# A hybrid recurrent layer on one core: odd heads' recurrence products leave TensorE by the upper partitions, and x's squares become two wide instructions

## The chip, the cores and the metric

The kernel runs on one core of a Trainium2 chip. The metric is device time in microseconds, from the start of the program to its end; for one core the slowest core is that core. A core has a matrix engine (TensorE; its weight loads are shown as PEld), a vector engine (VectorE, DVE), a scalar engine (ScalarE, ACT), GpSimd (POOL) and a queue engine (SyncE, SP) that issues DMAs. TensorE writes to PSUM, an accumulator memory of 128 partitions; VectorE and ScalarE copy results from there to SBUF, the working memory, also with 128 partitions. Taking a result out of PSUM is called an eviction below.

## What is computed

One layer (DEPTH is 1) over 512 tokens with 1024 channels. The input is normalised by its root mean square, projected to 6,920 columns, and four token mixers of width 256 run on parts of that projection: gated DeltaNet (GDN), RG-LRU, an S5 state-space layer and RWKV-7. Their outputs are gated, merged, projected and added to x; an MLP with squared ReLU and a final norm follow. What matters here are the norm and the two recurrences over chunks of 64 tokens with four heads of width 64:

```python
def _rmsnorm(x, g):
    y = x32 * lax.rsqrt(jnp.mean(x32 * x32, axis=-1, keepdims=True) + EPS)

# GDN, per chunk
def step(state, inp):
    u_i, w_i, q_i, k_i, a_i, gl_i = inp
    v_new = u_i - jnp.einsum("bhck,bhkv->bhcv", w_i, state)
    o = jnp.einsum("bhck,bhkv->bhcv", q_i, state) + jnp.einsum("bhcj,bhjv->bhcv", a_i, v_new)
    state = state * jnp.exp(gl_i)[..., None, None] + jnp.einsum("bhck,bhcv->bhkv", k_i, v_new)
    return state, o

# RWKV-7, per token (the kernel does it per chunk, too)
def step(state, inp):
    removed = jnp.einsum("bhvk,bhk->bhv", state, kk_t)
    state = (state * w_t[:, :, None, :]
             - jnp.einsum("bhv,bhk->bhvk", removed, kk_t * a_t)
             + jnp.einsum("bhv,bhk->bhvk", v_t, k_t))
    return state, jnp.einsum("bhvk,bhk->bhv", state, r_t)
```

## The kernel before

**Weights and projections.** All weights come as 134 units of 128x1024 fp32. `unit` (L316) loads one, and splits it into a high and a low part: ScalarE writes `hi` as fp32r (L333), VectorE writes `lo`, the rest (L334). `gemm` (L337) then makes each product of three fp32r matmuls (high by high, high by low, low by high). A projection of 128 columns (`proj`, L413) is 24 matmuls of 128x512 into one PSUM bank (`acc`); `nproj` (L419) evicts it on VectorE, scaled by the norm's row `N1["rs"]`. The first six accumulators use banks of their own (EARLY, L222), so that the first projections can be computed before the norm's factor is known.

**The norm.** `norm1` (L406) splits the eight 128x512 tiles of x by `split_g` (L382: `hi` on ScalarE, `lo` on VectorE) and calls `norm_stat` (L345). That squares each tile on ScalarE (L350), adds each square to a sum on VectorE (L354, L357), sums over the partitions by four matmuls with a column of ones (`ssa`, L368; each shows as two instructions), takes the root and the reciprocal (L372, L373), and spreads the result over partitions (`rsa`, L378). Its argument `parts` is 1 in the only call, so `keep_warm` does nothing.

**The RWKV recurrence** (`rwkv_r`, L670) runs over eight chunks. For chunk c, with `rr` the lower or upper 64 partitions for even or odd c: `r1` (L682; called `r` in the profile) multiplies the state `sv` of each head by `ab`, VectorE copies it (L685); `us` (L689) multiplies that by the inverted triangle `tf`, VectorE evicts it negated into the lower half of `uv` (L691), whose upper half is a ScalarE copy of `sv` (L686); `sn` (L696) gives the update of the state, VectorE adds the old state (L697) and multiplies by the decay (L698) into the state of the next chunk; `oT` (L703, L704) gives the output, copied by ScalarE (L705). In `oT` the even heads write the lower 64 partitions and the odd heads the upper 64. In r1, us and sn all four heads write the same 64 partitions, at different columns.

**The GDN recurrence** (`gdn_r`, L930) is built alike: `vn` (L960) and its VectorE copy into `sn` (L963), a ScalarE copy of the state into the other half (L964), the decayed state `sg_` (L967), `sg` (L971) and its addition into the next state (L972), and `oTg` (L977), copied by ScalarE (L978). Here vn and sg write the 64 partitions `rr` for all four heads. The last chunk has no sn, respectively sg.

**Other groups that the text below names.** `s5v` (L1287) are the S5 layer's products with a contraction over 128 partitions, 64 output partitions and 64 columns, whose outputs alternate between lower and upper 64 partitions from one matmul to the next. `s1g` (L916) are GDN's products of keys and queries within a chunk: 64 partitions contracted, 128 columns moving, outputs alternating between the halves. `tri_inverse` (L442) inverts the chunks' triangles: it writes them to DRAM and reads them back in another layout (`scrr` and `scrg`), twice, with a chain of 30 small VectorE instructions between, and has small matmuls of 16 or 32 partitions (`zp`, `t1p`, `z2p`, `z3p`).

**Order.** The PLAN (L68) lists the steps; each has a level of priority and a set of PSUM banks (LV, L63): RWKV's steps and the norm are at level 0, GDN's and S5's at 2. Weight units have a priority of their own, ahead of all levels (L320). From these the framework writes one fixed queue per engine, at build time; an engine works through its queue in order, so an instruction that waits holds up all behind it on that engine.

**Places.** Temporary tiles lie in five regions of SBUF. `al` (L138) gives a tile the place that HOME (L23) names for it, if that is free and of the right type, and otherwise the place that has been free for longest. Two tiles that share a place one after the other are ordered by that: the later one waits for the last reader of the earlier.

Of the kernel before, what the change touches and what calls it, by code (L numbers as in the profile page):

```python
# [22 lines left out]
HOME = {n: [(a[:a.index(":")], int(a[a.index(":") + 1:])) for a in v.split(",")] for n, v in (e.split("=") for e in """  # L23
    xt0=c1b:0 xgh=c0:0 xgl=c0:128 sqa0=c3:650 sqa1=c3:64 sqa2=c3:333 sqa3=c3:618 sqa4=c3:558 sqa5=c1a:81 sqa6=c3:634
    sqa7=c2:185 rsa=c3:202 zero=c2:43,c1b:78 wa=c3:514 gd=c3:64
    px=c2:52,c2:205,c3:383,c3:112,c3:218,c1a:105,c1b:0,c3:488,c3:526,c1b:16,c3:298,c1b:112,c3:525,c1b:16,c2:0,c1b:16
    reset=c3:542 kr=c1b:32 yk=c2:178 svr=c3:0 ab=c2:43 ccb=c1a:59 kf=c3:96,c1a:17 sig=c1b:96,c3:112 af=c3:466,c1b:96
    ei=c1b:112,c1a:0 eia=c1a:80,c3:558 wt=c1a:63,c3:447 bigwup=c3:325 hsbk=c1b:16,c3:298 rf=c3:80,c3:423
    vf=c3:333,c1b:112 rb=c3:349,c3:321 ntr=c1a:64 a2=c3:439 biggup=c2:242 s5s=c3:314 s5pol=c3:134 s5p=c1a:41
    bst=c1a:33 bsx=c2:8 bs2=c3:610 bs3=c3:530 c1=c1a:51 c2=c2:0 bigsb=c3:234 bigsbs=c3:666 bigsc=c2:16 bigscs=c1a:97  # L30
    b8=c3:358 s5t=c3:218,c3:610 s5u=c1a:96 s5ug=c3:325 s5h=c1a:0 lrow=c3:509 gsm=c2:250 ctri=c3:504 qk=c3:96,c3:391
    cv=c1b:0,c3:542,c1b:0,c1b:96,c1a:32,c1a:32 gv=c3:359 lu=c3:542 lh=c1b:96 lr=c1b:0,c1b:16 li=c3:509,c1b:0
    la2=c3:298,c3:298 biglwa=c2:27 biglwx=c2:35 lge=c3:526,c1b:16 c8=c3:218 t8w=c3:138 s5ct=c3:574 s5st=c3:590
    s5am=c2:18 s5ph=c2:175 s5tb=c3:282 s5a=c3:540 s5b=c3:503 s5hs=c3:290 cmr=c3:606 tfr=c2:0 bk=c3:610 s5y=c3:513
    s5yf=c3:326 s5yo=c3:514 bigglu=c1a:48 sgm=c3:290,c3:306 nbr=c1b:87 tnr=c3:128 tmr=c1b:70 tpr=c1b:32 t0tr=c2:210
    ztr=c1b:32 t11tr=c3:574 z2r=c1a:32 ktok=c2:176 ksqg=c1b:64 gpk=c3:136 grows=c3:130 gr=c1a:64 br=c1a:96 eg=c1a:0
    cneg=c2:173 cmg=c2:171 kx=c1b:64 kd=c3:250 svg=c2:176 aq=c3:546 tw=c3:324 ntg=c1a:0 tfg=c3:291 nbg=c1a:40
    tng=c2:35 tmg=c1a:112 tpg=c1a:32 t0tg=c1a:80 ztg=c1a:32 t11tg=c1a:64 z2g=c1a:112
    gt=c1b:0,c1b:0,c1b:16,c3:178,c1b:16,c3:178,c1b:16,c1b:16,c1b:0,c1b:48,c1b:16,c3:185,c1b:16,c1b:16,c3:170,c2:59,c3:234,c1b:0,c3:218,c3:610,c1b:0,c1b:48,c2:75,c2:176,c3:32,c2:0,c3:186,c1b:96,c2:42,c3:513,c1b:16,c2:125,c3:23,c2:32,c3:610,c3:626,c1b:0,c3:580,c3:598,c3:626,c3:337,c3:16,c3:136,c3:64,c3:594,c3:80,c3:626,c3:317
    ofr=c3:128 r1=c3:282,c1b:0,c1b:48,c3:194,c1b:40,c1b:40,c3:505,c1b:40  # L40
    uv=c1b:48,c1b:40,c1b:56,c3:503,c3:168,c3:160,c3:177,c2:34
    sm=c1b:8,c3:194,c1b:40,c3:185,c3:503,c3:168,c3:160,c1b:56 ofg=c2:143
    sn=c3:282,c3:473,c2:117,c3:282,c3:160,c1b:32,c2:92,c3:316
    sgs=c1b:32,c1b:40,c1b:75,c3:315,c3:473,c1b:75,c3:282,c1b:88 osq=c3:658,c3:626 hsbv=c2:16,c3:16 yh1=c1a:32
    yl1=c1a:64 mg=c3:456,c3:497,c3:170,c3:0,c3:48,c3:481,c3:658,c3:234 yh2=c1a:0 yl2=c1a:96 gz=c3:64 q2=c3:530,c1b:112
    o2=c2:240,c3:186 hsbo=c1b:96,c3:513 yh3=c1a:64 yl3=c1a:32 yh0=c1a:96 yl0=c1a:0
    x2=c3:107,c3:642,c3:423,c3:388,c3:407,c3:372,c3:439,c3:290 mh=c2:0 ml=c2:128 h2h=c0:0 h2l=c0:128 sqb0=c3:64
    sqb1=c3:610 sqb2=c3:32 sqb3=c3:0 sqb4=c3:16 sqb5=c3:48 sqb6=c3:531 sqb7=c3:626 rsb=c3:332
    dh=c1a:0,c1b:0,c2:128,c2:0 dl=c2:128,c2:0,c1a:0,c1b:0
    rl=c3:658,c3:0,c3:573,c3:626,c3:20,c3:46,c3:255,c3:0,c3:626,c3:0,c3:594,c3:16,c3:32,c3:56,c3:0,c3:16,c3:16,c3:626,c3:0,c3:32,c3:16,c3:626,c3:156,c3:658,c3:626,c3:610,c3:594,c3:503,c3:626,c3:16,c3:658,c3:0  # L50
    hc0=c3:497 hc1=c3:578 hc2=c3:184 hc3=c3:626 hc4=c3:658 hc5=c3:200 hc6=c3:481 hc7=c3:34 sqc0=c3:513 sqc1=c3:610
    sqc2=c3:236 sqc3=c3:16 sqc4=c3:533 sqc5=c3:610 sqc6=c3:562 sqc7=c3:594 rsc=c3:0
""".split())}
# [47 lines left out]
def trunk(ctx, tc, order, xT, wall, w8, prm, big, cst, gfr, out):  # L101
# [240 lines left out]
                mm(o, a[:, k0 + k, :], b[:, k, :], first and n == 0, last and n == 3 * nk - 1)  # L342
                n += 1

    def norm_stat(xt, nm, parts=1):  # L345
# [13 lines left out]
        def keep_warm(n, t):  # L359
            if parts > 1:  # L360
                w = pa("warm")
                for _ in range(n):
                    mm(w[:, 0:128], ones, t[:, 0:128])
# [2 lines left out]
        for i, acc in enumerate(accs):
            for u in range(4):
                mm(o[:, u:u + 1], acc[:, u * 128:u * 128 + 128], one, i + u == 0, i == parts - 1 and u == 3)  # L368
            keep_warm(3, acc)
        fr(*accs)  # L370
# [559 lines left out]
    def gdn_r():  # L930
# [22 lines left out]
        for c in range(8):  # L953
# [9 lines left out]
            V.tensor_copy(out=sn[rr], in_=o3[rr])  # L963
# [858 lines left out]
```

## Time and profile before

| what | us |
|---|---|
| median of the three runs | 883.51 |
| the three runs | 1213.66, 883.51, 882.94 |
| the profiled execution | 878.68 |
| its span (first instruction to last) | 876.9 |
| granted TensorE clock, mean over the span | 0.991 |

Engine times are sums of busy time within the span. TensorE's busy share counts an instruction until its modelled end, and neighbouring matmuls overlap, so a busy share near 100% doesn't mean that matmuls are as close as they can be; for that the starts of neighbouring matmuls are compared. A matmul on fp32 data (not fp32r) shows as two instructions, with two weight loads. In the timeline a row stands for several equal instructions: start of the first, time from there to the end of the last, count, and in brackets the idle time before and what ended it. The rows of a tile show shortest, median and longest duration in ns. The rows of groups show busy us, mean ns of one, and idle time before.

### The profile page before, as it was taken

What the parts mean: (1) busy time and instruction counts of PE and PEld (TensorE: products, weight loads), DVE (VectorE), ACT (ScalarE), POOL (GpSimd) and SP (SyncE); (2) the same over time, 40 slices, a digit from 0 to 9 for tenths busy, and PEclk for the clock granted to TensorE, in tenths of its full rate; (3) what the DMA queues carried; (4) which work ended last, traced back from release to release, by engine and by line L of the source; (5) the groups of instructions that cost most, each with busy time, mean ns of one, the idle gap of its engine ahead of it and who ended that gap; (6) DMA issues with size and microseconds to landing.
All of it is one profiled execution on the core that took longest, in us unless ns stands there. A gap on an engine that the chain in (4) does not pass through costs nothing.

```text
span 876.9 us, 12992 instructions
## 1 busy us (share of the span) xinstructions
PE 855.5 (98%) x5175; PEld 688.8 (79%) x5175; DVE 549.2 (63%) x967; ACT 422.8 (48%) x584; POOL 26.1 (3%) x38
## 2 busy tenths in 40 slices
PE   8999999998999899999999999999999999999996
PEld 6777777777777787777888788888888888888885
DVE  6899796993776258636655652454437553868553
ACT  8735557854522273333433333765545443644433
POOL 1000000000000000000000000000100110010000
PEclk9999999999999799999999999999999999999999
DMA  8433345455465652244323232556665877463302
GB/s 296 135 107 110 108 112 116 96 154 150 123 178 151 180 171 73 83 134 117 96 92 102 77 131 96 192 145 173 164 194 159 246 169 200 159 137 104 120 25 96
DMA packets 79292, 119.96 MB, mean 137 GB/s; under 512 B 42544, under 2 KB 49392, under 8 KB 79216
## 3 DMA queue, kind: packets, MB, share of 16 engines
q1 hardware_dynamic: 51968, 100.40, 35.4%
q0 software_dynamic: 3456, 12.58, 8.3%
q10 hardware_dynamic: 23808, 6.16, 3.3%
q8 instruction: 40, 0.66, 0.3%
q14 instruction: 20, 0.16, 0.1%
HBM read 103.79 MB, written 13.17 MB: 133 GB/s over the span
## 4 chain that ended last, share of the span: by engine, by line
PE 79%; DVE 7%; DMA 7%; ACT 4%; issue 2%; SPq 1%; ACTq 0%; DVEq 0%
PE acc L114 24%; PE facc L114 20%; PE dacc L114 17%; PE oacc L114 5%; PE bacc L114 4%; DVE c L120 2%; DMA c1a<-scrg 1%; DVE lo L120 1%; DMA c1a<-gscr 1%; ACT c L117 1%; PE s L114 1%; DMA raw<-in_wall_dram 1%; DVE c L129 1%; ACT L117 1%; DVE c1a L120 1%
## 5 line engine op out<-in xcount | busy, mean ns | idle before, releaser
L114 PE MATMUL acc<-c,hi 128*128 128x512 f32 x864 | 278.3, 400 | 3.7 <-DVE c L129 2.5
L117 ACT ACTIVATE hi<-raw 128x1024 fp32r<-128x1024 f32 x113 | 119.4, 1058 | 239.0 <-PE facc L114 73.5
L120 DVE TENSOR_TENSOR lo<-raw,hi 128x1024 fp32r<-128x1024 f32 x113 | 137.9, 1221 | 118.4 <-ACT hi L117 118.3
L114 PEld LDWEIGHTS acc<-c,hi 128*128 128x128 f32 x864 | 161.6, 190 | 44.4 <-DVE c L129 5.0
L114 PE MATMUL acc<-c,lo 128*128 128x512 f32 x432 | 173.9, 404 | 1.4 <-DVE lo L120 1.4
L114 PE MATMUL facc<-c,hi 128*128 128x512 f32 x336 | 103.4, 389 | 0.0
L114 PEld LDWEIGHTS acc<-c,lo 128*128 128x128 f32 x432 | 81.9, 190 | 20.6 <-DVE lo L120 2.0
L114 PEld LDWEIGHTS facc<-c,hi 128*128 128x128 f32 x336 | 63.1, 188 | 13.1
L117 ACT ACTIVATE c<-c 128x512 f32<-128x512 f32 (+5 forms) x101 | 63.9, 638 | 18.5 <-DVE c L120 11.8
L120 DVE TENSOR_TENSOR c<-c 128x16 f32<-128x16 f32 (+8 forms) x125 | 65.1, 534 | 4.2 <-ACT c L117 3.8
L114 PE MATMUL facc<-c,lo 128*128 128x512 f32 x168 | 65.5, 390 | 0.0
L114 PE MATMUL facc<-c,c1a 128*128 128x512 f32 x264 | 62.8, 391 | 0.0
L114 PE MATMUL dacc<-hi,c 128*128 128x512 f32 x176 | 57.4, 389 | 0.0
L114 PEld LDWEIGHTS facc<-c,c1a 128*128 128x128 f32 x264 | 49.3, 188 | 10.1
L117 ACT ACT_TABLE_LOAD x41 | 52.6, 1283 | 8.5 <-DMA raw<-in_wall_dram 3.0
L120 DVE TENSOR_TENSOR c<-acc,c 128x512 f32<-128x512 f32 x33 | 22.6, 687 | 45.4 <-PE acc L114 45.1
L120 DVE TENSOR_TENSOR c1a<-raw,c1a 128x1024 fp32r<-128x1024 f32 x21 | 25.7, 1223 | 32.7 <-ACT c1a L117 32.6
L114 PE MATMUL bacc<-c1a,hi 128*128 128x512 f32 x128 | 40.6, 401 | 0.0
L114 PE MATMUL oacc<-c,hi 128*128 128x512 f32 x128 | 39.8, 392 | 0.1
L117 ACT ACTIVATE c1a<-raw 128x1024 fp32r<-128x1024 f32 x21 | 22.2, 1058 | 36.5 <-PE facc L114 29.0
L114 PEld LDWEIGHTS dacc<-hi,c 128*128 128x128 f32 x176 | 33.0, 188 | 6.8
L114 PEld LDWEIGHTS facc<-c,lo 128*128 128x128 f32 x168 | 31.5, 188 | 6.5
(390 smaller groups left out, 1194.4 us busy)
## 6 DMA issues: line engine op xcount, KB each, us to landing
raw<-in_wall_dram SPq DMA_DIRECT2D x134, 512.0 KB, 3.5
...
```

Of the source, the lines that this page charges most:

```text
L114: P.matmul(out=o, lhsT=l, rhs=r, start=start, stop=stop)
L117: A.activation(out=o, in_=i, func=f, scale=scale, bias=bias)
L120: e.tensor_tensor(out=o, in0=a, in1=b, op=op)
L129: V.scalar_tensor_tensor(out=o, in0=a, scalar=s, in1=b, op0=op0, op1=op1)
```

## The change

Three things change.

1. In both recurrences, `r1`, `us`, `sn` and `vn`, `sg` write the products of heads 0 and 2 to the lower 64 partitions of the bank and those of heads 1 and 3 to the upper 64. The evictions are split by that: for r1, us and vn, VectorE takes the even heads and ScalarE the odd ones; for sn and sg, VectorE takes both in two instructions. The evictions move the data to the same partitions of the same tiles as before.
2. `norm_stat` squares x in two ScalarE instructions of 128x2048 (even and odd tiles), adds the two, and folds the sum twice (1024, then 512 columns), all on VectorE. The matmuls behind it are as before. The two tiles `swa0`, `swa1` have no entry in HOME.
3. Many entries of HOME change, most of them places of small tiles (256 or 512 columns). Order, priorities and the PLAN stay as they are.

```diff
-    def norm_stat(xt, nm, parts=1):
-        accs = []
-        for k in range(8):
-            sq = t2(f"sq{nm}{k}")
-            act(sq, xt[k], ACT.Square)
-            if k == 0 or k == 7:
-                accs.append(sq)
-            else:
-                tt(V, accs[-1], accs[-1], sq, ADD)
-                fr(sq)
-        while len(accs) > parts:
-            tt(V, accs[-2], accs[-2], accs[-1], ADD)
-            fr(accs.pop())
...
+    def norm_stat(xt, nm):
+        sq_ = [t8(f"sw{nm}{e}") for e in range(2)]
+        sq = [v3(t, 4) for t in sq_]
+        for e in range(2):
+            act(sq[e], v3(xt, 8)[:, e:8:2], ACT.Square)
+        tt(V, sq_[0], sq_[0], sq_[1], ADD)
+        fr(sq_[1])
+        for n in (1024, 512):
+            tt(V, sq_[0][:, 0:n], sq_[0][:, 0:n], sq_[0][:, n:2 * n], ADD)
         o = ps("ss" + nm)
...
+    def half(h):
+        return slice(64 * (h % 2), 64 * (h % 2) + 64)
...
             for h in range(4):
-                mm(o3[rr, h, :], ab[:, c, h, 0, :], sv[:, c, h, :])
+                mm(o3[half(h), h, :], ab[:, c, h, 0, :], sv[:, c, h, :])
...
-            V.tensor_copy(out=r1[rr], in_=o3[rr])
+            V.tensor_copy(out=r1[rr, 0:4:2], in_=o3[half(0), 0:4:2])
+            A.copy(out=r1[rr, 1:4:2], in_=o3[half(1), 1:4:2])
...
-                mm(o3[0:64, h, :], tf4[rr, u, h, :], r1[rr, h, :])
-            ts(V, uv[0:64], o3[0:64], -1.0, MUL)
+                mm(o3[half(h), h, :], tf4[rr, u, h, :], r1[rr, h, :])
+            ts(V, uv[0:64, 0:4:2], o3[half(0), 0:4:2], -1.0, MUL)
+            act(uv[0:64, 1:4:2], o3[half(1), 1:4:2], ACT.Copy, -1.0)
...
-                    mm(o3[0:64, h, :], bk4[:, c, h, :], uv[:, h, :])
-                tt(V, sm[0:64], o3[0:64], sv[0:64, c], ADD)
+                    mm(o3[half(h), h, :], bk4[:, c, h, :], uv[:, h, :])
+                for e in range(2):
+                    tt(V, sm[0:64, e:4:2], o3[half(e), e:4:2], sv[0:64, c, e:4:2], ADD)
...
-                mm(o3[rr, h, :], tw4[:, c, h, :], sv[:, c, h, :])
+                mm(o3[half(h), h, :], tw4[:, c, h, :], sv[:, c, h, :])
...
-            V.tensor_copy(out=sn[rr], in_=o3[rr])
+            V.tensor_copy(out=sn[rr, 0:4:2], in_=o3[half(0), 0:4:2])
+            A.copy(out=sn[rr, 1:4:2], in_=o3[half(1), 1:4:2])
...
-                    mm(o3[rr, h, :], kd4[rr, u, h, :], sn[rr, h, :])
-                tt(V, sv[rr, c + 1], o3[rr], sg_[rr], ADD)
+                    mm(o3[half(h), h, :], kd4[rr, u, h, :], sn[rr, h, :])
+                for e in range(2):
+                    tt(V, sv[rr, c + 1, e:4:2], o3[half(e), e:4:2], sg_[rr, e:4:2], ADD)
```

A line of HOME before and after, as an example of the third part:

```diff
-    uv=c1b:48,c1b:40,c1b:56,c3:503,c3:168,c3:160,c3:177,c2:34
+    uv=c1a:8,c1b:40,c1b:56,c3:503,c3:168,c3:160,c3:177,c2:34
```

More of the change, by code (lines that the diff above doesn't have):

```diff
@@ L23 @@
 HOME = {n: [(a[:a.index(":")], int(a[a.index(":") + 1:])) for a in v.split(",")] for n, v in (e.split("=") for e in """
-    xt0=c1b:0 xgh=c0:0 xgl=c0:128 sqa0=c3:650 sqa1=c3:64 sqa2=c3:333 sqa3=c3:618 sqa4=c3:558 sqa5=c1a:81 sqa6=c3:634
-    sqa7=c2:185 rsa=c3:202 zero=c2:43,c1b:78 wa=c3:514 gd=c3:64
+    xt0=c1b:0 xgh=c0:0 xgl=c0:128 sqa0=c3:212 sqa1=c3:17 sqa2=c3:250 sqa3=c2:16 sqa4=c1a:48 sqa5=c3:332 sqa6=c3:642
+    sqa7=c3:217 rsa=c3:202 zero=c1b:96,c1a:31 wa=c3:514 gd=c3:64
     px=c2:52,c2:205,c3:383,c3:112,c3:218,c1a:105,c1b:0,c3:488,c3:526,c1b:16,c3:298,c1b:112,c3:525,c1b:16,c2:0,c1b:16
-    reset=c3:542 kr=c1b:32 yk=c2:178 svr=c3:0 ab=c2:43 ccb=c1a:59 kf=c3:96,c1a:17 sig=c1b:96,c3:112 af=c3:466,c1b:96
@@ L28 @@
[L28 to L37, printed above, removed]
@@ L38 @@
-    tng=c2:35 tmg=c1a:112 tpg=c1a:32 t0tg=c1a:80 ztg=c1a:32 t11tg=c1a:64 z2g=c1a:112
-    gt=c1b:0,c1b:0,c1b:16,c3:178,c1b:16,c3:178,c1b:16,c1b:16,c1b:0,c1b:48,c1b:16,c3:185,c1b:16,c1b:16,c3:170,c2:59,c3:234,c1b:0,c3:218,c3:610,c1b:0,c1b:48,c2:75,c2:176,c3:32,c2:0,c3:186,c1b:96,c2:42,c3:513,c1b:16,c2:125,c3:23,c2:32,c3:610,c3:626,c1b:0,c3:580,c3:598,c3:626,c3:337,c3:16,c3:136,c3:64,c3:594,c3:80,c3:626,c3:317
-    ofr=c3:128 r1=c3:282,c1b:0,c1b:48,c3:194,c1b:40,c1b:40,c3:505,c1b:40
-    uv=c1b:48,c1b:40,c1b:56,c3:503,c3:168,c3:160,c3:177,c2:34
@@ L42 @@
[L42 to L52, printed above, removed]
+    reset=c3:594 kr=c1b:32 yk=c2:178 svr=c3:565 ab=c2:43 ccb=c1a:59 kf=c3:96,c1a:17 sig=c3:243,c3:112 af=c3:466,c1b:96
@@ new lines @@
+    ei=c1b:112,c1a:0 eia=c1a:80,c3:558 wt=c1a:63,c3:447 bigwup=c3:325 hsbk=c1b:16,c3:145 rf=c3:80,c3:423
+    vf=c3:333,c1b:112 rb=c3:349,c3:321 ntr=c1a:64 a2=c1a:89 biggup=c2:242 s5s=c3:314 s5pol=c3:134 s5p=c1a:41
+    bst=c3:191 bsx=c2:8 bs2=c1a:80 bs3=c2:35 c1=c1a:51 c2=c1a:53 bigsb=c3:234 bigsbs=c1b:32 bigsc=c2:16 bigscs=c1a:97
+    b8=c2:143 s5t=c3:218,c3:610 s5u=c1a:96 s5ug=c3:325 s5h=c1a:0 lrow=c3:509 gsm=c3:128 ctri=c1b:85 qk=c3:96,c3:391
+    cv=c1b:0,c3:542,c1b:0,c3:381,c1a:32,c1a:32 gv=c3:359 lu=c3:542 lh=c1b:96 lr=c2:143,c1b:16 li=c3:509,c1b:0
@@ new lines @@
+    la2=c3:298,c3:298 biglwa=c2:27 biglwx=c2:35 lge=c3:526,c1b:16 c8=c3:218 t8w=c3:91 s5ct=c1b:89 s5st=c3:138
+    s5am=c1b:57 s5ph=c1a:98 s5tb=c3:282 s5a=c3:218 s5b=c2:38 s5hs=c3:290 cmr=c3:391 tfr=c3:112 bk=c3:510 s5y=c3:513
+    s5yf=c3:326 s5yo=c3:514 bigglu=c1a:48 sgm=c3:290,c3:306 nbr=c1b:87 tnr=c2:35 tmr=c1b:70 tpr=c1a:76 t0tr=c2:210
+    ztr=c1b:32 t11tr=c3:574 z2r=c1a:32 ktok=c2:176 ksqg=c1b:64 gpk=c1b:83 grows=c3:15 gr=c1a:64 br=c1a:96 eg=c3:387
+    cneg=c1a:96 cmg=c1b:112 kx=c1b:64 kd=c3:250 svg=c2:176 aq=c3:546 tw=c3:324 ntg=c1a:0 tfg=c3:291 nbg=c1a:40
@@ new lines @@
+    tng=c2:35 tmg=c1a:112 tpg=c1a:32 t0tg=c1a:80 ztg=c1a:32 t11tg=c1a:64 z2g=c1a:112
+    gt=c1b:0,c1b:0,c3:397,c3:178,c1b:16,c3:178,c1b:16,c1b:16,c1b:0,c1b:48,c1b:16,c3:185,c1b:16,c1b:16,c3:170,c2:59,c3:234,c1b:0,c3:218,c3:610,c1b:0,c1b:48,c2:75,c2:176,c3:32,c2:0,c3:186,c1b:96,c2:42,c3:513,c1b:16,c2:125,c3:23,c2:32,c3:610,c3:626,c1b:0,c3:580,c3:598,c3:626,c3:337,c3:16,c3:136,c3:64,c3:594,c3:80,c3:626,c3:317
+    ofr=c3:610 r1=c3:282,c1b:0,c3:306,c3:194,c1b:40,c1b:40,c3:505,c1b:40
+    uv=c1a:8,c1b:40,c1b:56,c3:503,c3:168,c3:160,c3:177,c2:34 sm=c1b:8,c3:194,c1b:40,c2:156,c3:503,c3:168,c3:160,c1b:56
@@ new lines @@
+    ofg=c2:128 sn=c3:282,c2:13,c2:117,c3:282,c3:160,c1b:32,c2:92,c3:316
+    sgs=c1b:32,c1b:40,c1b:75,c3:315,c3:473,c3:466,c3:282,c2:35 osq=c3:558,c3:145 hsbv=c2:16,c3:16 yh1=c1b:70 yl1=c2:16
+    mg=c3:456,c1a:108,c3:45,c1a:40,c3:48,c3:481,c3:481,c3:234 yh2=c3:600 yl2=c3:586 gz=c3:239 q2=c3:530,c1b:112
+    o2=c3:612,c3:32 hsbo=c3:349,c3:321 yh3=c1a:32 yl3=c1b:76 yh0=c1b:64 yl0=c1a:84
+    x2=c3:107,c3:391,c3:423,c1a:22,c3:407,c1a:32,c3:439,c3:290 mh=c2:0 ml=c2:128 h2h=c0:0 h2l=c0:128 sqb0=c3:64
@@ new lines @@
+    sqb1=c3:560 sqb2=c1b:93 sqb3=c3:91 sqb4=c2:169 sqb5=c3:447 sqb6=c3:183 sqb7=c3:447 rsb=c3:523
+    dh=c2:193,c3:538,c1a:0,c1a:96 dl=c2:190,c2:0,c3:234,c1b:0
+    rl=c3:658,c3:243,c3:573,c3:626,c3:20,c3:46,c3:255,c3:0,c3:626,c3:250,c3:594,c3:16,c3:32,c3:56,c3:642,c3:16,c3:16,c3:626,c3:0,c3:32,c3:16,c3:626,c3:156,c3:658,c3:626,c3:610,c1a:98,c3:503,c3:469,c3:16,c3:658,c1b:20
+    hc0=c3:571 hc1=c3:503 hc2=c3:347 hc3=c1a:32 hc4=c1a:41 hc5=c1b:112 hc6=c3:191 hc7=c3:504 sqc0=c3:256 sqc1=c2:193
+    sqc2=c1a:68 sqc3=c1b:6 sqc4=c1a:67 sqc5=c2:16 sqc6=c2:22 sqc7=c3:183 rsc=c3:177
@@ L343, in gemm @@
                 n += 1
-    def norm_stat(xt, nm, parts=1):
-        accs = []
-        for k in range(8):
-            sq = t2(f"sq{nm}{k}")
-            act(sq, xt[k], ACT.Square)
-            if k == 0 or k == 7:
-                accs.append(sq)
-            else:
-                tt(V, accs[-1], accs[-1], sq, ADD)
-                fr(sq)
-        while len(accs) > parts:
-            tt(V, accs[-2], accs[-2], accs[-1], ADD)
-            fr(accs.pop())
[L359 to L363, printed above, removed]
-        o = ps("ss" + nm)
[L366 to L370, printed above, removed]
+    def norm_stat(xt, nm):
[7 more added lines that the diff above has]
+            tt(V, sq_[0][:, 0:n], sq_[0][:, 0:n], sq_[0][:, n:2 * n], ADD)
+        o = ps("ss" + nm)
+        for u in range(4):
+            mm(o[:, u:u + 1], sq_[0][:, u * 128:u * 128 + 128], one, u == 0, u == 3)
+        fr(sq_[0])
         st = sm_.tile([128, 4], F, name="st" + nm)
@@ L409, in norm1 @@
             split_g(xs[k], "g1", k, xgh[:, k, :], xgl[:, k, :])
-        N1["rs"] = norm_stat(xs, "a")
+        N1["rs"] = norm_stat(xt, "a")
         fr(xt)
```

## Prediction

> **What bounds the kernel now.** I read the page first (spans, slices, chain), then the busy time by stretch, then TensorE's timeline around both recurrences and at the start.
>
> ```profile
> span 876.9 us, 12992 instructions
> PE 855.5 (98%) x5175; PEld 688.8 (79%) x5175; DVE 549.2 (63%) x967; ACT 422.8 (48%) x584; POOL 26.1 (3%) x38
> PE 79%; DVE 7%; DMA 7%; ACT 4%; issue 2%; SPq 1%; ACTq 0%; DVEq 0%
> ```
>
> TensorE is busy for 98% of the span and carries 79% of the chain that ended last. No other engine is above 63%. By stretch (length, busy us and count of PE, PEld, DVE, ACT, POOL, granted clock, DMA share, GB/s):
>
> ```profile
> 0.00:16.00 16.00, 12.62 (x48) 9.41 (x49) 9.95 (x27) 11.76 (x19) 2.90 (x11) 1.00 0.87 319
> 230.00:290.00 60.00, 57.97 (x403) 43.87 (x402) 36.74 (x79) 19.02 (x27) 0.00 (x0) 1.00 0.59 153
> 290.00:320.00 30.00, 28.20 (x635) 23.93 (x636) 13.38 (x24) 9.87 (x19) 0.00 (x0) 0.83 0.51 166
> 333.00:420.00 87.00, 85.76 (x498) 67.03 (x497) 51.83 (x79) 28.50 (x43) 1.88 (x2) 1.00 0.37 111
> ```
>
> The RWKV recurrence runs from about 218 to 319 us, the GDN one from 333 to 418. In both TensorE is hardly idle, because projection matmuls lie between the chunk's steps in its queue. So TensorE time that a step gives up is time won, unless a wait for something else stands right behind it.
>
> **Recurrence groups: the matmuls.** Each chunk has groups of four fp32 matmuls, one per head, and each matmul is two instructions in the trace. Today all four heads of a group write the same 64 partitions.
>
> ```profile
> 279.73 0.68 PE L114 MATMUL sn<-c 128*64 128x64 f32 x8
> 382.75 0.68 PE L114 MATMUL sg<-c 64*64 64x64 f32 x8
> 111.39 0.92 PE L114 MATMUL s5v<-c 128*64 128x64 f32 x24
> 232.19 1.59 PE L114 MATMUL s1g<-c 64*64 64x128 f32 x32
> L114 PE MATMUL sn<-c x32: 222/222/368, 279.7 to 315.4; 128*64 128x64 f32 x32
> L114 PE MATMUL vn<-c,c x64: 222/222/270, 333.2 to 412.6; 128*64 128x64 f32 x64
> ```
>
> A group of 8 takes 0.68 us from first start to last end, and the last instruction takes 0.222 (median of the tile's row): (0.68 - 0.222)/7 = 65 ns from one start to the next. s5v (L1287) has the same shape, but its output alternates between lower and upper 64 partitions with every matmul: (0.92 - 0.222)/23 = 30 ns. That is exactly what the change makes of r1, sn and vn. For us and sg, which contract over 64 partitions that stay the same for the whole group, the near row is s1g: it also keeps its 64 rows, alternates the output half, and goes at (1.59 - 0.28)/31 = 42 ns, with 128 columns moving instead of 64. So 42 is the upper end there, 30 the lower.
>
> Count: vn stands at x64 = 8 chunks x 4 heads x 2, so 8 groups. By the loops r1 and us also have 8, and sn and sg 7 (no last chunk): 38 groups. One saves 7 x (65 - 30) = 0.245 us, in all 9.3 us. With 42 ns for the 15 groups of us and sg: 15 x 7 x 0.012 = 1.3 less, 8.0. I take 30: s1g's extra is most simply its wider moving operand.
>
> The Trainium skill ("TensorE: Matmul & The Clock Gate", Part 3, what overlaps and what doesn't) says that a weight load runs beside a matmul in flight only where the row group differs. These groups keep their rows and change the columns alone, so by that sentence nothing is gained here and the sum would hold only the start's term. The trace disagrees: s5v uses all 128 rows, changes only the output half, and goes at 30 ns.
>
> **What of it is lost.** Six of the 38 groups lie ahead of a wait that TensorE's speed does not move:
>
> ```profile
> 256.57 5.91 DMA scrg<-c1a
> 284.90 6.50 DMA c1a<-scrg
> 285.17 0.68 PE L114 MATMUL r<-c,c 128*64 128x64 f32 x8
> 288.54 0.24 PE L114 MATMUL zpg<-c1a 16*32 16x16 f32 x4 [1.33 <-DMA c1a<-scrg]
> 291.44 0.41 PE L114 MATMUL zpg<-c1a 16*32 16x16 f32 x14 [1.31 <-DMA c1a<-scrg]
> 291.78 1.11 PE L114 MATMUL us<-c1b,c 64*64 64x64 f32 x8
> 297.54 1.05 PE L114 MATMUL acc<-c,hi 128*128 128x512 f32 x2
> 301.06 0.62 PE L114 MATMUL acc<-c,hi 128*128 128x512 f32 x2
> ```
>
> GDN's triangular inverse goes to DRAM and back from 256.57 (write) to 291.40 (last read). Groups between those times (us, sn of chunk 2, r1, us, sn of chunk 3, r1 of chunk 4) only lengthen that wait, unless other projection work moves up. I count them lost: 6 x 0.245 = 1.5 us. Left: 9.3 - 1.5 = 7.8.
>
> **Recurrence groups: the evictions.**
>
> ```profile
> L120 DVE TENSOR_TENSOR c<-s,c 64x256 f32<-64x256 f32 x24 | 9.5, 422 | 0.2
> L120 DVE TENSOR_TENSOR c1a<-s,c 64x128 f32<-64x128 f32 x16 | 4.5, 282 | 2.1 <-PE s L114 1.8
> L978 ACT COPY c<-oTg 128x128 f32<-128x128 f32 x8 | 2.1, 267 | 12.7 <-PE oTg L114 12.6
> 376.25 0.68 PE L114 MATMUL vn<-c,c 128*64 128x64 f32 x8
> 376.35 1.28 ACT L117 ACT_TABLE_LOAD   x1
> 377.51 0.41 DVE L963 COPY c<-vn 64x256 f32<-64x256 f32 x1
> 381.55 1.06 ACT L117 ACTIVATE hi<-raw 128x1024 fp32r<-128x1024 f32 x1 [3.27 <-issue]
> ```
>
> r1, us and vn: one VectorE instruction of 64x256 (422 ns) becomes one VectorE of 64x128 (282) and one ScalarE of half the size (about 267), side by side: 24 new ScalarE instructions, 24 x 0.27 = 6.4 us, on an engine that is busy 28.50 of 87 us there. VectorE gives up 24 x 0.14 = 3.4 us. sn and sg: one of 422 becomes two of 282, 14 x 0.14 = 2.0 us more on VectorE. I cost all of it at nothing on the path: between a group and its reader lie projection matmuls, as from vn at 376.25 (read by the copy at 377.51) to sg at 382.75, 6.5 us. If that cover is gone, a late ScalarE costs TensorE the wait itself (a rival below). Queued behind the new ScalarE copies are the next unit's splits (hi<-raw), which today start with idle time ahead of them (3.27 us in the row).
>
> **The start: x's squares.**
>
> ```profile
> 7.75 1.41 DVE L129 SCALAR_TENSOR_TENSOR c<-c1b,pr,c 128x512 fp32r<-128x512 f32 x2
> 9.08 0.69 DVE L120 TENSOR_TENSOR c<-c 128x512 f32<-128x512 f32 x1
> 16.23 0.74 DVE L129 SCALAR_TENSOR_TENSOR c<-c1b,pr,c 128x512 fp32r<-128x512 f32 x1
> 8.55 0.50 PE L114 MATMUL acc<-c,hi 128*128 128x512 f32 x1 [0.81 <-DVE c L129]
> 11.75 0.50 PE L114 MATMUL acc<-c,hi 128*128 128x512 f32 x1 [0.30 <-DVE c L129]
> 15.77 0.50 PE L114 MATMUL acc<-c,hi 128*128 128x512 f32 x1 [0.52 <-DVE c L129]
> 15.56 1.05 ACT L117 ACTIVATE hi<-raw 128x1024 fp32r<-128x1024 f32 x1
> 17.73 0.96 PE L114 MATMUL ssa<-one,c 128*128 128x1 f32 x8
> 28.13 1.28 DVE L120 TENSOR_TENSOR c<-acc,c 128x512 f32<-128x512 f32 x2
> 581.27 5.44 PE dacc L114 x24
> ```
>
> The first projection is paced by VectorE: between two splits of x (0.74) stands the sum of a square (0.69), so the last low part runs from 16.23 to 16.97, and TensorE waits at each; its first unit ends with the matmul behind that, near 17.2. A matmul of 512 columns costs 5.44/24 = 0.227 us. With wide squares, which need all of x, the eight low parts follow one another at 1.41/2, under 0.7 us: the last ends at about 7.75 + 8 x 0.67 = 13.1. TensorE then goes at three matmuls (0.68) a part, and its first unit ends near 8.55 + 23 x 0.227 = 13.8, 3.4 earlier. The next unit's split now competes with two squares of 2048 columns (1.05 per 1024, so about 2.1 each, from 11.4 on): behind one of them it would run from 13.5 to 14.6, an idle 0.8. Gain 3.4 - 0.8 = 2.6; without that idle 3.4; with both squares first (split done at 16.7, idle 2.9) 0.5. I take 2.6, as the code gives weight splits the higher priority (L320) and one square may already run when the weights land. (The 11.4 is an estimate: ScalarE now does sixteen splits and squares by 15.56, the first from 6.5 on; eight of them end about half-way, and a little later for x's arrival.) The sums stay as long (2048, 1024 and 512 columns for seven of 512), and the statistic comes some 2 us later; nothing reads it before the first scaling at 28 us, and six accumulators are open by then.
>
> **Places.** Costs no instruction; it moves waits between tiles that share a place. No row prices it. I take 0 and leave both signs to the rivals.
>
> **Sum.** 876.9 - 7.8 - 2.6 = 866.5 us of span. 1.8 us lie around it (878.68 for the profiled execution), so 868.3. The median of the runs (883.51) is 4.8 above the profiled execution; the forecast on that scale is 873.1, say 873, 1.2% under before. From about 2% a measurement of this kernel can be told from no change, so the likeliest verdict is "no change".
>
> **Rivals.**
>
> *The halves do not overlap* (the skill's rule above). Then only the start is won: 883.5 - 2.6 = 881. s5v and s1g speak against it. Chance 0.10.
>
> *ScalarE's late half (slower).* ScalarE works in order; a copy that falls behind a weight split (1.06) or a table load (1.28) is late by that, and us and sg wait for both halves. Place: the 24 split evictions. With one split in front of each and no cover, 24 x 1.06 = 25 us, less the 10.4 won: 898; with a table load (24 x 1.28) 904. It turns the sign from 10.4/24 = 0.43 us of wait per eviction. For it: at 376.35 a table load stands just where vn's copy would go. Against it: 6.5 us of cover there. Chance 0.08.
>
> *A wait more, with the slow clock behind it.* The order of all queues is set anew. The waits at 288.54 and 291.44 show the price of one bad place: 1.33 + 1.31 idle, then small groups at 1.11 instead of 0.68 and a pair of projection matmuls at 1.05 instead of 0.62 until 301: 2.6 + about 1 + 6 x 0.43, some 6 us. One more of these: 879; two, 885. For it: round trips through DRAM carry much of the chain between 145 and 290:
>
> ```profile
> 197.67 5.93 DMA c<-c1a
> ...
> 211.13 7.00 DMA c1a<-gscr
> ```
>
> Chance 0.14.
>
> *A wait fewer.* The same 6 us won, with the better places: 867; with the full 9.3 and 3.4 as well, 865; two fewer, 860. Chance 0.18.
>
> **How the numbers follow.** The forecast as it stands has 0.50, its own range 868 to 879 (its bounds: 38 groups at 8.0 to 9.3 less 0 to 1.5, the start 0.5 to 3.4, which is 871 to 877, and the runs' own scatter). Over 2% faster means under 865.8: most of "a wait fewer" is just above it; I give 0.14. Over 2% slower means above 901.2: part of the ScalarE rival, two waits more with it, 0.06. Within 2%: 0.80. The range 860 to 886 leaves out the ScalarE rival and the outer ends.
>
> **What would show it.** In the profile after: groups r, us, sn, vn, sg of 8 at about 0.43 us instead of 0.68 (right) or still 0.68 (the first rival); the eight low parts of x back to back, and ssa about as far along although later in TensorE's work; the first unit ending before 14.5. ScalarE's half evictions named as releasers of us or sg with more than 0.4 us of TensorE idle would be the second rival; idle and a granted clock under 0.9 in a new stretch the third. The forecast is wrong if TensorE's busy time in these groups falls by 8 us and the span doesn't: then the stretch from 145 to 330 is bound by VectorE and the round trips through DRAM.

## The result and the profile after

| kernel | median us of 8 runs | ratio to before, 95% interval |
|---|---|---|
| before | 881.47 | |
| changed | 889.11 | 1.009 [1.0061, 1.0118] |

The changed kernel is 7.6 us slower, where 10 us less were forecast. At a bound of 2% this is still "no change", but it lies outside the range given (860 to 886). The profiled execution after took 890.12 us, with a span of 888.3. One of the eight executions of before (1213.66 us) was a slow one; the ratio is of the others.

The page of the changed kernel (span; busy time; the granted clock in 40 slices of 22 us; the chain that ended last):

```profile
span 888.3 us, 13013 instructions
PE 862.4 (97%) x5175; PEld 693.6 (78%) x5175; DVE 548.7 (62%) x977; ACT 423.3 (48%) x598; POOL 26.3 (3%) x38
PEclk9999999997999859999999999999999999999999
PE 84%; DMA 5%; ACT 4%; DVE 4%; issue 1%; SPq 1%; POOL 0%; ACTq 0%; DVEq 0%; POOLq 0%
```

TensorE executes as many instructions as before (x5175), yet it is busy 6.9 us longer, and the clock shows holes in slices 10, 14 and 15 (200 to 222 and 289 to 333 us). First the groups themselves, in TensorE's timeline of the changed kernel:

```profile
264.53 0.45 PE L113 MATMUL us<-c1b,c 64*64 64x64 f32 x8
303.94 0.45 PE L113 MATMUL r<-c,c 128*64 128x64 f32 x8
333.24 0.45 PE L113 MATMUL vn<-c,c 128*64 128x64 f32 x8
319.94 0.69 PE L113 MATMUL r<-c,c 128*64 128x64 f32 x8
```

A group takes 0.45 us where it took 0.68, and us is as fast as r. The last row is the same group at half clock: 0.69. So the gain is there, and something takes it back. The table of stretches tells where (columns: stretch, length, busy us and count of PE, PEld, DVE, ACT, POOL, granted clock, DMA share, GB/s). The kernel before:

```profile
0.00:40.00 40.00, 36.49 (x152) 27.41 (x153) 30.35 (x137) 30.91 (x50) 2.90 (x11) 1.00 0.72 237
130.00:220.00 90.00, 84.95 (x818) 66.80 (x816) 66.88 (x161) 58.50 (x77) 0.13 (x1) 0.98 0.53 129
220.00:340.00 120.00, 116.17 (x1253) 92.36 (x1253) 72.64 (x140) 47.89 (x76) 0.00 (x0) 0.96 0.52 151
340.00:430.00 90.00, 88.76 (x496) 69.54 (x495) 51.54 (x76) 31.55 (x46) 1.88 (x2) 1.00 0.36 109
```

The changed kernel:

```profile
0.00:40.00 40.00, 34.23 (x153) 27.57 (x154) 29.54 (x127) 23.14 (x36) 3.15 (x11) 0.96 0.70 233
130.00:220.00 90.00, 83.29 (x678) 67.50 (x681) 66.23 (x165) 51.13 (x69) 1.95 (x2) 0.94 0.45 114
220.00:340.00 120.00, 114.79 (x1366) 89.28 (x1357) 67.50 (x144) 51.73 (x93) 0.31 (x1) 0.86 0.51 143
340.00:430.00 90.00, 89.76 (x523) 70.78 (x520) 58.60 (x97) 39.52 (x62) 1.87 (x2) 1.00 0.44 135
```

Read each row as a loss: idle time (length less PE busy) and, at a granted clock under 1, that share of the busy time. From 220 to 340 us, before: 3.8 idle and about 0.04 x 116 = 4.6 lost to the clock; after: 5.2 idle and 0.14 x 115 = 16. The first 40 us lose more, too (3.5 before; 5.8 + 0.04 x 34 = 7.1 after); but 1.1 us of that lie before 7.2 us, where TensorE waits for x and the kernel before filled the time with warm-up matmuls.

The records of the clock know two values, 1.00 and 0.50, so this can be summed over the whole span: idle = span less PE busy; clock loss = half of the PE busy time inside the stretches at 0.50 (13.7 us of such stretches before, 47.8 us after, without the idle tail of the program); the rest is what would be left at full clock. The clock loss is an upper figure. From one matmul of 512 columns to the next it is 0.43 us at half clock and 0.23 at full, nearly twice, but a small group takes 0.69 instead of 0.45.

| profiled execution of | span | idle | clock loss, at most | rest, at least |
|---|---|---|---|---|
| before | 876.9 | 21.4 | 6.3 | 849.2 |
| changed | 888.3 | 25.9 | 22.6 | 839.8 |
| halves alone (e2) | 875.6 | 23.2 | 8.4 | 844.0 |
| wide squares alone (e3) | 895.0 | 29.6 | 17.3 | 848.1 |
| new places alone (e4) | 905.8 | 35.0 | 27.3 | 843.4 |
| halves and wide squares (e13) | 885.4 | 31.5 | 12.9 | 840.9 |
| halves and a later factor (e15) | 883.9 | 30.1 | 11.7 | 842.1 |

The changed kernel's rest fell by 9.4 us, and idle time (+4.5) and the half clock (+16.3) took it back: 876.9 - 9.4 + 4.5 + 16.3 = 888.3. That this is near the gross gain of 9.3 that the prediction worked out for the groups is chance. e4, whose groups are those of before, is down by 5.8, because the clock loss is overstated where much ran at half clock. Priced by kind of matmul (its distance to the next at half clock, less the median distance of the same pair at full clock), the half clock costs 5.7 us before and 19.1 after, so some 13 more, and the rest falls by 6.5.

The groups themselves can be summed directly, from the first start of each part to the start of what follows (or to its own end, if that is earlier): 23.3 us before, 18.3 in the changed kernel (where more of them ran at half clock) and 16.5 in e2. So the halves take 5 to 7 us from TensorE, not 9.3. Many groups are no longer whole: in e2 five of eight us and four of seven sn run in parts with projection matmuls between, head 0 as soon as VectorE's half is there and the other three behind ScalarE's. An us group of e2:

```profile
226.65 0.33 PE L114 MATMUL us<-c,c 64*64 64x64 f32 x2
226.91 0.73 PE L114 MATMUL acc<-c,hi 128*128 128x512 f32 x2
227.57 0.44 PE L114 MATMUL us<-c,c 64*64 64x64 f32 x6
```

To the next matmul the two parts take 0.26 + 0.37 = 0.63 us, as much as the whole group before (0.60); a whole group takes 0.38.

### The profile page after: what moved, and what is told of

It is laid out like the page before. It is cut to its first block, busy times and chain, and to the rows that moved or that the text cites. A ratio compares the mean times of both kernels' runs of the same rounds, so it can differ in the third digit from the quotient of the medians.

```text
span 888.3 us, 13013 instructions
## 1 busy us (share of the span) xinstructions
PE 862.4 (97%) x5175; PEld 693.6 (78%) x5175; DVE 548.7 (62%) x977; ACT 423.3 (48%) x598; POOL 26.3 (3%) x38
## 4 chain that ended last, share of the span: by engine, by line
PE 84%; DMA 5%; ACT 4%; DVE 4%; issue 1%; SPq 1%; POOL 0%; ACTq 0%; DVEq 0%; POOLq 0%
PE acc L113 26%; PE facc L113 20%; PE dacc L113 17%; PE bacc L113 5%; PE oacc L113 5%; DMA c1a<-scrg 1%; PE s5y L113 1%; DVE c1a L119 1%; PE s L113 1%; DMA c1a<-gscr 1%; ACT c L116 1%; ACT hi L116 1%; ACT L116 1%; DVE c L119 1%; DVE c L128 1%
## 5 line engine op out<-in xcount | busy, mean ns | idle before, releaser
L113 PE MATMUL acc<-c,hi 128*128 128x512 f32 x864 | 282.5, 405 | 4.9 <-ACT hi L116 2.3
L113 PEld LDWEIGHTS acc<-c,hi 128*128 128x128 f32 x864 | 164.3, 193 | 45.9 <-issue 5.2
L119 DVE TENSOR_TENSOR c<-c 128x16 f32<-128x16 f32 (+8 forms) x118 | 59.7, 523 | 1.9 <-ACT c L116 1.5
L113 PE MATMUL dacc<-hi,c 128*128 128x512 f32 x160 | 52.6, 389 | 0.0
L119 DVE TENSOR_TENSOR c1a<-raw,c1a 128x1024 fp32r<-128x1024 f32 x21 | 25.7, 1224 | 32.7 <-ACT c1a L116 32.6
L113 PE MATMUL dacc<-hi,c1b 128*128 128x512 f32 x112 | 37.1, 389 | 0.0
```

The lines of the kernel that those rows point to most:

```text
L113: P.matmul(out=o, lhsT=l, rhs=r, start=start, stop=stop)
L119: e.tensor_tensor(out=o, in0=a, in1=b, op=op)
```

## The experiments

**Each part by itself.** e2 has only the first part of the diff, e3 only the new `norm_stat`, e4 only the new HOME, e1 everything but the new `norm_stat`.

> The changed kernel with the squares of before (eight of 512 columns, each added as it comes); the halves and the new places stay. Theory N (the wide squares bring the norm's factor 7 us later, the RWKV steps follow 20 us later, and the last chunks then meet no projections and run at half clock): time falls to at or under the kernel before, 870 to 881, with rsa near 25 us and less than 20 us of half clock. Theory E (ScalarE's half of an eviction starts only when VectorE's half has ended, or behind other work, and this stretches the recurrence): still slower than before, 884 to 892. Theory P (places): still slower, 884 to 892.

> The kernel before with the split halves alone; squares and places as before. Theory N: 870 to 879, TensorE's groups shorter and nothing lost. Theory E: slower than before, 884 to 892, with TensorE waiting for the evictions of us and r in the last chunks. Theory P: 870 to 879.

> The kernel before with the two wide squares alone. Theory N: slower than before by 4 to 12 us, with the RWKV recurrence some 15 to 20 us later and more half clock. Theory E: within 3 us of before. Theory P: within 3 us of before.

> The kernel before with the new places alone. Theory N and theory E: within 3 us of before. Theory P (tiles that now share a place wait for each other): slower than before by 4 to 12 us.

| kernel | median us | ratio to before, 95% interval |
|---|---|---|
| e2, halves alone | 878.15 | 0.9962 [0.9935, 0.9989] |
| e3, wide squares alone | 896.22 | 1.0154 [1.0117, 1.0191] |
| e4, new places alone | 905.16 | 1.0255 [1.0208, 1.0302] |
| e1, halves and new places | 901.94 | 1.0228 [1.0201, 1.0254] |

The halves win 3.3 us; each of the other two loses, by 15 and 24 us, and the three don't add up to the 7.6 of the whole. e1 missed all its expectations: with the squares of before put back, the changed kernel is not faster but some 12 us slower. So what the wide squares cost hangs on the places: 15 us in e3, and with the new places the kernel that has them is the faster one. In each of these slow kernels RWKV's inverse starts late. VectorE's first and last reduction of its 15 steps and the first matmul behind them, before:

```profile
137.19 0.15 DVE L459 TENSOR_REDUCE c<-c1b 128x1 f32<-128x1 f32 x1
163.30 0.38 DVE L459 TENSOR_REDUCE c<-c1b 128x15 f32<-128x225 f32 x1
...
171.71 0.24 PE L114 MATMUL zpr<-c,c1a 16*32 16x16 f32 x4 [0.73 <-DMA c<-scrr]
```

and in the changed kernel:

```profile
159.89 0.15 DVE L447 TENSOR_REDUCE c<-c 128x1 f32<-128x1 f32 x1
195.55 0.39 DVE L447 TENSOR_REDUCE c<-c 128x15 f32<-128x225 f32 x1
...
206.66 0.24 PE L113 MATMUL zpr<-c,c1a 16*32 16x16 f32 x4
```

The steps begin 23 us later and take 36 us instead of 26. zpr is at 200.9 in e3, 209.4 in e4 and 172.2 in e2. The next runs looked for the cause of that.

**Which place makes the inverse late?** With the new HOME, the tile `bk` finds its place taken and falls to columns that S5's tables `st` and `am` used; its copies by ScalarE wait for S5's scan (185.27 instead of 153.55 us). e5 (the changed kernel) and e6 (e4) give these tables memory of their own, with their old places still reserved, so that no other tile moves:

```diff
-        ct, st, am = t2("s5ct"), t2("s5st"), t2("s5am")
+        ct, *own = t2("s5ct"), t2("s5st"), t2("s5am")
+        st, am = (wp.tile([128, 512], F, name=n) for n in ("st_own", "am_own"))
```

> The changed kernel, but the S5 tables st and am lie in memory of their own; their old places stay reserved, so every other tile keeps its place. Theory P (with the new places bk falls back to a place whose last user is the S5 tables, so its four copies wait for S5's scan at 185 us, RWKV's inverse starts 35 us later, and the recurrence runs 20 us later, where few projections are left): copies of bkT at 155 to 170 us, inverse (zpr) at 175 to 190, under 30 us of half clock, time 876 to 885. Theory N (the late norm factor alone): zpr still after 200, 886 to 892.

> The kernel before with the new places and the S5 tables st and am in memory of their own. Theory P: copies of bkT at 155 to 165, zpr at 172 to 185, and most of the 24 us of the places come back: 880 to 890. Against it: 900 to 908.

Measured: 886.54 (1.0081 [1.0049, 1.0113]) and 914.71 (1.0395 [1.0358, 1.0432]). The copies of bk went back to 139 to 163 and 135 to 161 us, but zpr stayed at 210 and 203. The theory fell. e9 (e4) and e11 (changed) do the same with two tiles of the inverse itself, which in the new order come to lie where S5's `bs3`, RG-LRU's `biglwx` and GDN's `lrow` lay:

```diff
         nb, tn, tn2, tmp = (t1(n + nm) for n in ("nb", "tn", "tm", "tp"))
+        homes = tn, tmp
+        if nm == "r":
+            tn, tmp = (wp.tile([128, 256], F, name=n) for n in ("tn_own", "tp_own"))
```

> The new places alone, as in the fourth kernel (905.2 us), but the two tiles tn and tp of RWKV's inverse lie in memory of their own; their places stay reserved, so that no other tile moves. Theory 'late inverse': with the new places tn takes over the columns of bs3 and biglwx and tp those of lrow and li, so VectorE's memset of tn is queued behind S5's readers (151.6 us) and the 15 steps begin at 159 though their data landed at 137. Then the steps should begin at 137 to 140, the first zpr stand at 168 to 178 (209 now, 172 before) and the time fall to 875 to 886. Rival 'slow clock': the places cost by what happens later, whatever the inverse does: zpr early, the time still 896 or more. Rival 'another place': the steps still begin at 155 or later and the time stays at 900 to 910.

> The changed kernel (889.1 us) with tn and tp of RWKV's inverse in memory of their own, nothing else moved. Theory 'late inverse' with two causes in series: the data still land at 150 to 153 because of the late factor, so the steps begin at 152 to 157 instead of 160, the first zpr stands at 198 to 208 and the time at 884 to 892. Rival 'places alone': the places are all that delays the inverse: zpr at 170 to 180 and the time at 868 to 880.

e9 took 909.83 (1.0323 [1.0281, 1.0366]), e11 891.31 (1.0109 [1.0078, 1.014]). In e9 the steps did begin on time, yet zpr did not: its other input is read back from DRAM into columns that the transposes for bk still read, and those wait for bk's copies:

```profile
138.61 0.14 DVE L461 TENSOR_REDUCE tn_own<-tp_own 128x1 f32<-128x1 f32 x1
161.42 0.38 DVE L461 TENSOR_REDUCE tn_own<-tp_own 128x15 f32<-128x225 f32 x1
...
201.86 0.57 ACT L663 COPY c<-bkT 128x512 f32<-128x512 f32 x1
...
206.85 0.24 PE L113 MATMUL zpr<-c,c1a 16*32 16x16 f32 x4
```

So at least two waits for places run side by side to nearly the same end, and taking either away shows the other. That is no accident of one tile. Followed through the program's order of allocations, the old HOME gives 289 of its 301 listed tiles the place listed, and the twelve others come late, in the MLP. The new one, in the program that it came with, gives 212 of 293; 81 find it taken (102 of 301 in e4). The first is `svr`: listed at c3:565 for 64 units of 32 columns, it would overlap `reset`, listed at c3:594 and alive. Those 81 lie where space has been free for longest, which nobody chose. In e4, which puts the list into a program for which it wasn't made, this costs 24 us. e1 has the same 102 misses and the same cost over e2, so it tests these places and not the wide squares.

**What makes the wide squares slow?** The factor is late. The changed kernel's ScalarE at the start:

```profile
10.78 1.90 ACT L116 ACTIVATE c1a<-c1b 128x2048 f32<-128x2048 f32 x1
12.59 0.70 ACT L116 ACTIVATE c<-c1b,pr 128x512 fp32r<-128x512 f32 x1
13.20 1.89 ACT L116 ACTIVATE c1a<-c1b 128x2048 f32<-128x2048 f32 x1
15.00 1.04 ACT L116 ACTIVATE hi<-raw 128x1024 fp32r<-128x1024 f32 x1
...
26.99 1.05 ACT L116 ACTIVATE hi<-raw 128x1024 fp32r<-128x1024 f32 x1
28.05 1.28 ACT L116 ACT_TABLE_LOAD   x1
29.35 0.26 ACT L116 ACTIVATE sta<-ssa,kcs 128x4 f32<-128x4 f32 x1
```

and its VectorE and TensorE:

```profile
15.12 2.29 DVE L119 TENSOR_TENSOR c1a<-c1a 128x2048 f32<-128x2048 f32 x1 [1.05 <-ACT c1a L116]
18.71 1.22 DVE L119 TENSOR_TENSOR c1a<-c1a 128x1024 f32<-128x1024 f32 x1
21.69 0.69 DVE L119 TENSOR_TENSOR c1a<-c1a 128x512 f32<-128x512 f32 x1
```

```profile
16.09 0.73 PE L113 MATMUL acc<-c,hi 128*128 128x512 f32 x2 [1.23 <-ACT hi L116]
17.92 1.22 PE L113 MATMUL acc<-c,hi 128*128 128x512 f32 x2 [1.09 <-ACT hi L116]
26.04 0.95 PE L113 MATMUL ssa<-one,c1a 128*128 128x1 f32 x8
31.97 1.05 PE L113 MATMUL rsa<-cs,sta 128*128 128x128 f32 x8
```

Before, the squares were summed beside the splits, and the last sum ended at 17.5. Now the three sums run one after the other with splits of the weights between them, until 22.3; the matmuls for the sum come at 26.04 (17.73 before), the root stands behind a split and a table load, and rsa is at 31.97 instead of 24.85. Both squares also run ahead of the second unit's split: TensorE waits 1.23 and 1.09 us and then goes at half clock for 3.4.

e8 (e3) gives the whole `norm_stat` an earlier priority. e10 (e3) and e12 (e11) let TensorE sum the two squares:

```diff
-        tt(V, sq_[0], sq_[0], sq_[1], ADD)
-        fr(sq_[1])
-        for n in (1024, 512):
-            tt(V, sq_[0][:, 0:n], sq_[0][:, 0:n], sq_[0][:, n:2 * n], ADD)
...
-        for u in range(4):
-            mm(o[:, u:u + 1], sq_[0][:, u * 128:u * 128 + 128], one, u == 0, u == 3)
+        for e in range(2):
+            for k in range(4):
+                for u in range(4):
+                    mm(o[:, u:u + 1], sq[e][:, k, u * 128:u * 128 + 128], one, e + k + u == 0, e + k + u == 7)
```

> The kernel before with the two wide squares, and squares, sums and factor of the norm ahead of the weight splits (priority -45000 instead of level 0). Theory N (the late factor costs the 15 us): factor (rsa) at 20 to 27 us instead of 33.6, zpr back at 172 to 185, time 880 to 887. Against it: 893 to 899 although the factor comes early.

> The wide squares alone, as in the third kernel (896.2 us), but the two square tiles are summed by 32 small matmuls on TensorE in place of three adds on VectorE and four matmuls. Theory 'late factor': with the adds the sum is ready at 22.4 (17.5 before), the root comes behind other work of ScalarE at 28.8 (20.2 before), the factor at 34 to 35 (26.3 before), and the data of the inverse land at 148 instead of 137. Without the adds the factor should come at 25 to 28, the data at 135 to 141, the first zpr at 165 to 178 (201 now), and the time fall to 874 to 884; the 28 further matmuls cost up to 3.4 us of that by the 0.12 us of one before. Rival 'start': the squares cost by TensorE's waits and half clock at 16 to 21 us, which stay: 892 to 898.

> The changed kernel with both: tn and tp in memory of their own, and the wide squares summed on TensorE. Theory 'late inverse': both causes are gone, the data land at 136 to 143, zpr stands at 170 to 185 and the time at 868 to 880, below the changed kernel's by 9 to 20 us. Rival 'slow clock' or any other cost of the new places: zpr early and the time still 885 or more.

Measured: e8 888.10 (1.0095 [1.0068, 1.0122]), e10 895.09 (1.0146 [1.011, 1.0181]), e12 898.04 (1.0185 [1.0149, 1.022]). None brought the factor forward: rsa at 32.3, 32.9 and 33.7. e8 won 8 us over e3 all the same, with almost the same queues. In e10 zpr was early (175.4), and the time was not: the first projections, with the small matmuls among them, ran at half clock for 13.7 us from 16.5 on. So an early inverse isn't enough, and e8, e10 and e12 tell nothing of an early factor.

**Do the two evictions hinder each other?** e7 (e2) stores heads 0 and 2 next to each other, and 1 and 3, so that the two engines write separate ranges.

```diff
-            V.tensor_copy(out=r1[rr, 0:4:2], in_=o3[half(0), 0:4:2])
-            A.copy(out=r1[rr, 1:4:2], in_=o3[half(1), 1:4:2])
+            V.tensor_copy(out=r1[rr, 0:2], in_=o3[half(0), 0:4:2])
+            A.copy(out=r1[rr, 2:4], in_=o3[half(1), 1:4:2])
```

> The kernel before with the split halves, heads 0 and 2 stored in the first half of the tiles r1, uv and sn and heads 1 and 3 in the second, so that the two evictions write ranges that don't interleave. Theory E (ScalarE's eviction waits for VectorE's because the written ranges interleave): the two start within 0.1 us of each other wherever ScalarE is free, and the time is 2 to 5 us under the split halves' 878: 873 to 876. Against it: the pairs still follow one another, or they don't and the time stays at 877 to 880, as the evictions are covered.

Measured: 878.64, as e2's 878.15; against the runs of before beside it that is 1.0016 [0.9984, 1.0048], so the halves' gain is at the edge of what is seen. But the two still run one after the other. In e7, too, ScalarE starts only when VectorE's half is done (VectorE 344.53 to 344.81, then):

```profile
344.85 0.26 ACT L975 COPY c<-vn 64x128 f32<-64x128 f32 x1 [2.98 <-DVE c L974]
```

What orders the two is a wait in the program, in e7 as in e2: each of these ScalarE copies waits for semaphore 100, which VectorE's instructions alone raise, and for the count that VectorE's half reaches; it doesn't wait for TensorE's semaphore (102) by itself. So the ranges written have nothing to do with it. Why the framework puts the wait there is open, and so is what an overlap would bring.

**A late factor without wide squares.** e13 is the changed kernel with the old HOME. e14 and e15 are e2 with the factor carried through one or two more small tiles by DMA:

```diff
         V.reciprocal(out=st, in_=st)
+        if nm == "a":
+            for i in range(2):
+                st_ = sm_.tile([128, 4], F, name=f"st{nm}{i}")
+                nc.gpsimd.dma_start(out=st_, in_=st)
+                st = st_
```

> The changed kernel without its new places: halves and wide squares, the places as before. Theory 'late factor': the squares cost the same 15 us as alone (896.2 against 881) and the halves give 3 us: 890 to 896, with the factor at 32 to 35, the inverse's data at 147 to 150, the first zpr at 198 to 208 and 25 us or more at half clock. The new places would then have taken off 1 to 7 us in the changed kernel (889.1), though alone they add 24. Rival 'places': the new places make the changed kernel slow, and without them it stands at 874 to 882.

> The halves alone (878.2 us), with nothing added but one copy by DMA of the norm's factor (128x4) to another small tile before it is used, which makes the factor later by one trip of 2 to 5 us. Theory 'late factor': the inverse's data land by about as much later (140 to 145 for 136.5), the steps take longer because other work of VectorE comes between them, and the time rises to 880 to 892. Rival 'harmless': nothing urgent hangs on the factor, the time stays at 876 to 880.

> The same with two such copies in a row, 4 to 10 us later, about what the wide squares make of it (8.7). Theory 'late factor': the inverse's data at 143 to 152, the first zpr at 195 to 210 (172 without), 30 us or more at half clock and the time at 888 to 905, as with the wide squares, although no square was touched. Rival 'harmless': 876 to 882, and the wide squares cost by something else.

| kernel | rsa at | zpr at | median us | ratio to before, 95% interval |
|---|---|---|---|---|
| e2, halves alone | 24.3 | 172.2 | 878.15 | 0.9962 [0.9935, 0.9989] |
| e14, factor later | 32.3 | 180.5 | 884.21 | 1.0037 [1.0017, 1.0058] |
| e15, factor later still | 33.7 | 202.9 | 885.12 | 1.0046 [1.0032, 1.006] |
| e13, halves and wide squares | 32.6 | 200.5 | 890.69 | 1.0112 [1.0082, 1.0142] |

The table of stretches of e15, then of e13:

```profile
0.00:40.00 40.00, 36.52 (x162) 29.19 (x163) 31.93 (x149) 25.98 (x45) 4.15 (x13) 1.00 0.73 237
130.00:220.00 90.00, 79.78 (x690) 63.47 (x689) 67.34 (x173) 53.17 (x72) 0.44 (x2) 0.92 0.55 129
220.00:340.00 120.00, 111.98 (x1312) 85.40 (x1311) 65.22 (x135) 52.20 (x86) 0.00 (x0) 0.93 0.54 148
```

```profile
0.00:40.00 40.00, 34.21 (x150) 27.54 (x151) 31.31 (x138) 24.78 (x37) 2.97 (x11) 0.96 0.71 237
220.00:340.00 120.00, 110.88 (x1374) 84.35 (x1364) 68.89 (x142) 54.04 (x92) 0.00 (x0) 0.94 0.51 148
```

With a factor 8 to 9.4 us later the kernel is 6 to 7 us slower (0.75 and 0.84% of before, with intervals apart from e2's), although no square is touched. The edit also sets the order of all queues anew. Since a mere reordering moved e3 to e8 by 8 us, two kernels of one sign support the theory rather than prove it. The expectation for e15 (888 to 905) was too high, and the trip took some 8 us once and only 1.5 more the second time. The loss isn't read from zpr: e14 has it 22 us earlier than e15 and is no faster. It appears as idle time and half clock between 130 and 340 us, as in the changed kernel. What the start adds is read at equal work: the 96th projection matmul, behind the same small ones, starts at 34.9 in e15, 37.6 in e13 and 37.0 in the changed kernel, so 2 to 3 us of the 5.6 between e13 and e15. (The profiled execution of e13, 887.17, was its fastest, 1.5 us above e15's.) And e13 without the new places is as fast as the changed kernel (890.69 and 889.11, ratios 1.0112 and 1.0090 with intervals that overlap): in the company of the wide squares the new places cost nothing that can be measured, although without them they cost 24 us (e4 against before, e1 against e2).

The fastest kernel that ran is e2, the halves without the rest: 0.38% under before.

## Why the prediction was wrong

- **Groups, -7.8.** Right in mechanism, too large in size. A whole group takes 0.45 us (0.43 was forecast), and us gains like r, so the rival that halves don't overlap fell. The Trainium skill ("TensorE: Matmul & The Clock Gate", Part 3) lets a weight load run beside a matmul only where the row group differs; the trace disagrees: in the kernel before, whose groups keep rows and columns, each load already starts while the matmul ahead of it runs, and where the columns alone change 0.68 becomes 0.45. The prediction counted 38 whole groups; in e2 nine of them break and gain next to nothing, so that the groups give up 6 to 7 us instead of 9.3. Of that, 3.3 reach the time.
- **Evictions, "at nothing on the path".** Not nothing: they are what breaks the groups. ScalarE's half waits for VectorE's instead of running beside it, and sometimes comes 3 us later behind other work. ScalarE, then TensorE, of the changed kernel:

```profile
323.67 2.09 ACT L931 COPY c<-c 64x1024 f32<-64x1024 f32 x2
325.79 0.27 ACT L116 ACTIVATE c<-us 64x128 f32<-64x128 f32 x1
```

```profile
324.31 0.47 PE L113 MATMUL sn<-c,c 128*64 128x64 f32 x2
326.11 0.58 PE L113 MATMUL sn<-c,c 128*64 128x64 f32 x5 [0.92 <-ACT c L116]
```

  That is the second rival in small. It didn't decide the sign: e2, with the same evictions, is faster than before.
- **Start, -2.6.** Wrong in sign. The first unit did end 3 us earlier (14.9 instead of 17.9; 13.8 was forecast). The prediction named the bad case (both squares ahead of the split) and still counted it as a gain of 0.5; that case came, and the half clock behind it. At equal work the term is +2 to +3.
- **"The statistic comes some 2 us later; nothing reads it before the first scaling at 28 us".** This is the step that failed. I counted VectorE's columns, which are as many as before, and not the queues that the sum, the root and the copy stand in: rsa came 7.1 us later, at 31.97 instead of 24.85, and the first scaling 8.4 us later, at 36.54 instead of 28.13. VectorE of the changed kernel:

```profile
36.54 1.88 DVE L119 TENSOR_TENSOR c<-acc,c 128x512 f32<-128x512 f32 x3
```

  By e14 and e15, whose first scalings come at 35.71 and 36.46, that is worth +6 to +7. This is argued from kernels with the old places; in the changed kernel itself nothing brought the factor forward without moving the places too.
- **Places, 0.** Not wrong for the whole (e13 against the changed kernel), but that is luck: the list could have been followed through the allocations beforehand, and would have shown that 81 entries don't take effect.
- **The rival "a wait more, with the slow clock behind it", 0.14.** This is how the loss arrived, and it held up in kind: short idles, each with a stretch at half clock behind it, +4.5 and +13 to +16 us in sum, about three of the 6 us that it set for one.

With the terms as the runs measured them the sum is: halves -3.3, factor +6 to +7, start +2 to +3, places about 0, in all +5 to +7; the changed kernel stands at +7.6, with an interval from +5.4 to +10.4. The terms are differences between kernels in which all queues were set anew, so the agreement is weak evidence. How a late factor becomes idle time from 130 on, through which of the queues, isn't settled: neither rsa nor zpr orders all the kernels by time.
